# One flag at the scheduler: the same instructions, ordered by a different simulation

## The chip, the cores and the metric

The program runs on one core of one Trainium2 chip, in one launch. The metric is the device time of one execution in microseconds (us). Lower is better. An execution has five instruction streams that matter here: TensorE (PE in the rows, with its weight loads as PEld), VectorE (DVE), ScalarE (ACT), GpSimd (POOL) and SyncE (SP), from which this kernel issues every transfer. Each stream is executed in the order in which it was written into the program; an instruction that waits holds back what stands behind it in its own stream.

## The reference, cut to what matters

One inference step of a two-layer decoder trunk, for a prompt of 1024 tokens and for 8 single-token samples that share the weights. All data is float32. Cut:

```python
def even_layer(hn, ...):                      # layer 0
    u = hn @ w_in                             # q|k|v|gate + z|xBC|dt
    o = dilated_attention(q, k, v)            # three windows: 128/1, 512/4, 2048/16
    att = o * silu(g_att)
    xbc = causal_conv(xbc, ...)               # 4 taps, silu
    y = ssd_scan(xs, dt, a, bm, cm, ...)      # chunks of 128 tokens, a state per head
    y = rmsnorm(y * silu(z))
    return concat([att, y]) @ w_out

def odd_layer(hn, ...):                       # layer 1
    u = hn @ w_in                             # q|k|v|o|i|f|z
    qk = causal_conv(q|k, ...)
    h = mlstm_chunked(q, k, v, i, logf, ...)  # chunks of 128 tokens, a 256x256 memory per head
    h = head_norm(sigmoid(o) * h)
    return (h * silu(z)) @ w_out

# x + even_layer(rmsnorm(x)), then + odd_layer(rmsnorm(.)), then a last rmsnorm;
# the sample tokens take one step each from their caches and states
```

## The kernel before, in words

Activations lie transposed, features on the 128 partitions and the 1032 tokens (1024 of the prompt and 8 samples) along the free axis. To keep float32 accuracy every large product is made of three matmuls: each operand is split into a rounded high part and a low part (`split`, L90: ScalarE casts the high part, VectorE or GpSimd subtracts to get the low part), and `mm3` (L104) adds high x high, high x low and low x high into one PSUM bank. Nearly all of TensorE's time goes into such triples.

PSUM has eight banks of 128x512: three belong to the tag "mm" (`MM`, L72, with `PS_MM = 3`) for the large projections, five to the tag "ax" (`X`, L75) for everything small. A bank is free again when ScalarE or VectorE has read the result.

The program is traced as straight-line code, in this order:

- **Layer 0.** After the first loads and the first norm come the q|k|v blocks (`pq`, 4 groups of 9 blocks), with attention pieces (`att_a`, `att_b`) put between them by hand; then 12 feature tiles through the convolution (`conv_c`, `conv_taps` L243, `conv_act`), then 12 gate tiles (`gate_c`, L228) with the 16 pieces of the state scan (`ssd_prep`, L722, and `ssd_main`) between them, then the output projection (`out_f`, L914) in two halves of the tokens.
- **Layer 1.** Eight heads in a loop (L1496). Each head has four q and k tiles through `conv_c` and two z tiles through `gate_c` (3 pieces of 344 tokens each, result tile `pf`), and then nine blocks: `vo_block` (L1445: 24 matmuls of 512 columns into `pvo`) followed by `mstage` (L1472), which makes the preparation of chunk c (`ml_prep`, L1265), the main part of chunk c-1 (`ml_main`, L1296) and the output of chunk c-2 (`ml_out`, L1330). During head 0 the scalar gates of all heads are made in steps (`gates_a` to `gates_f`), which the loop drops between the projection pieces. Then comes the second output projection and the last norm.

`ml_main` carries the chain from chunk to chunk: the matmuls `mC` give the update of the memory `Cst` (VectorE, L1318), ScalarE rounds it to `mCh` (L91), GpSimd makes the low part `mCl` (L92), and the matmuls `mN` of the next chunk read both:

```python
        if c < 7:
            hd["Cs"] = (R("mCh", [128, 2, VC], 1), R("mCl", [128, 2, VC], 1))
            split(*hd["Cs"], Cst, G)
```

Weights come through the class `Weights` (L116): a transfer into one of three buffers `raw`, a cast `wh` on ScalarE (L91) and a subtraction `wl` on GpSimd or VectorE (L92). `wv_fetch` (L1439) does the same for the v and o weights (`wvh`, `wvl`, the low part always on GpSimd).

What sets the order of the work: the traced order is only the wish. When the block `with tile.TileContext(nc)` closes, a list scheduler plays the whole program through on a simulated machine. Whenever an engine of that machine is free, the scheduler gives it, among the instructions whose inputs are there and for whose tiles a buffer is free at that moment of the simulation, the one that was traced first. The order in which each engine took its instructions becomes the stream of the real engine, and buffers are handed out in the same sequence. So an instruction is moved behind a later-traced one only if the simulated machine finds it not ready. The simulated machine of the kernel before takes the durations of instructions from a static table.

## Time and profile before

| | |
|---|---|
| Time, median of 3 runs | 2216.33 us (2213.23 to 2218.28) |
| The profiled execution's own time | 2213.76 us |
| its span, first to last instruction | 2211.7 us |
| TensorE busy | 2117.2 us of the span (96%) |
| weight loads (PEld) busy | 1890.8 us (85%) |
| VectorE, ScalarE, GpSimd busy | 62%, 38%, 39% |
| mean granted clock of TensorE | 0.986 |
| moved by DMA | 232.29 MB, 105 GB/s |

The span is what the profiler saw between the first and the last instruction; the execution's own time is 2.1 us longer. Matmul records overlap (the engine is pipelined), so "busy" says that at least one matmul was under way, not that the engine ran at its peak. The granted clock is 1.00 where TensorE ran at 2.4 GHz throughout, and falls toward 0.50 in stretches where it ran at 1.2 GHz.

### The profile page before, as it was taken

To read this page: it belongs to the slowest core of one execution; us is meant where nothing else is said; L and a number is where in the kernel's file an instruction comes from. 1 tells how busy PE (TensorE), PEld (TensorE's weight loads), DVE (VectorE), ACT (ScalarE), POOL (GpSimd) and SP (SyncE) were. 2 spreads that over 40 slices of the span, in tenths; PEclk is the share of its full clock that TensorE was granted. 3 is DMA by queue.
4 is the path that set the end of the run, shared out by engine and by line. 5 is a ranking of instruction groups with operands and counts; after the bars stand their busy time and mean duration, and the time that the engine had idled before them with its cause. 6 is when DMAs were issued, how large, how long until landed. Compare 5 with 4: busy or idle time off the path is not lost. (4 is left out here: it accounts for less than half of the span.)

```text
span 2211.7 us, 35220 instructions
## 1 busy us (share of the span) xinstructions
PE 2117.2 (96%) x12913; PEld 1890.8 (85%) x12913; DVE 1381.0 (62%) x3075; ACT 845.4 (38%) x1828; POOL 857.7 (39%) x1167
## 2 busy tenths in 40 slices
PE   7999989998999999899999999999999999999998
PEld 6877777997898798789988889898898988987798
DVE  7344488678877545644648566576575664856854
ACT  5434434454434323433424334243343342523331
POOL 4222152115543343343444435434354344542321
PEclk9999999999999999999999999999999999999999
DMA  4222142325555551411213223132241232415753
GB/s 156 70 73 76 52 145 73 93 71 174 166 183 185 159 175 40 94 37 48 88 33 109 77 89 123 36 102 82 75 138 28 84 104 61 139 38 187 256 179 101
DMA packets 161918, 232.29 MB, mean 105 GB/s; under 512 B 41170, under 2 KB 106690, under 8 KB 161746
## 3 DMA queue, kind: packets, MB, share of 16 engines
q1 hardware_dynamic: 161746, 230.04, 33.2%
q8 instruction: 102, 1.67, 0.3%
q14 instruction: 70, 0.57, 0.1%
HBM read 174.35 MB, written 55.62 MB: 104 GB/s over the span
## 5 line engine op out<-in xcount | busy, mean ns | idle before, releaser
L113 PE MATMUL pf<-yh,wh 128*128 128x344 f32 x1152 | 375.5, 326 | 11.9 <-ACT gth L232 11.0
L113 PE MATMUL pf<-yl,wh 128*128 128x344 f32 x1152 | 372.7, 323 | 1.7 <-POOL yl L92 1.7
L113 PE MATMUL pf<-yh,wl 128*128 128x344 f32 x1152 | 371.5, 323 | 0.3 <-DVE wl L92 0.3
L92 POOL TENSOR_TENSOR wl<-raw,wh 128x1024 fp32r<-128x1024 f32 x86 | 214.6, 2495 | 353.6 <-ACT wh L91 353.6
L113 PEld LDWEIGHTS pf<-yh,wh 128*128 128x128 f32 x1152 | 219.6, 191 | 16.6 <-ACT gth L232 13.5
L113 PEld LDWEIGHTS pf<-yl,wh 128*128 128x128 f32 x1152 | 219.6, 191 | 2.6 <-POOL yl L92 2.6
L113 PEld LDWEIGHTS pf<-yh,wl 128*128 128x128 f32 x1152 | 219.2, 190 | 0.8 <-DVE wl L92 0.7
L246 DVE SCALAR_TENSOR_TENSOR cout<-craw,mcw,cout 128x1024 f32<-128x1024 f32 x96 | 145.7, 1518 | 114.7 <-ACT cout L244 113.1
L91 ACT CAST wh<-raw 128x1024 fp32r<-128x1024 f32 x128 | 134.1, 1048 | 207.6 <-PE po L927 82.0
L113 PE MATMUL pvo<-wvh,yh 128*128 128x512 f32 x512 | 205.8, 402 | 0.0
L113 PE MATMUL pvo<-wvl,yh 128*128 128x512 f32 x512 | 201.7, 394 | 0.0
L113 PE MATMUL pvo<-wvh,yl 128*128 128x512 f32 x512 | 201.6, 394 | 0.0
L113 PE MATMUL pf<-xh,wh 128*128 128x344 f32 x576 | 195.8, 340 | 2.7 <-ACT gth L232 2.7
L113 PE MATMUL pf<-xl,wh 128*128 128x344 f32 x576 | 188.0, 326 | 0.0
L113 PE MATMUL pf<-xh,wl 128*128 128x344 f32 x576 | 187.7, 326 | 0.0
L1263 DVE TENSOR_SCALAR mx<-mx,mbs,md 128x256 f32<-128x256 f32 x64 | 26.4, 413 | 178.0 <-POOL md L1262 178.0
L927 PE MATMUL po<-oh,wl 128*128 128x512 f32 (+2 forms) x384 | 123.6, 322 | 5.2 <-DVE wl L92 4.2
L927 PE MATMUL po<-oh,wh 128*128 128x512 f32 (+2 forms) x384 | 123.9, 324 | 1.0 <-ACT oh L91 1.0
L927 PE MATMUL po<-ol,wh 128*128 128x512 f32 (+2 forms) x384 | 123.1, 321 | 0.0
L113 PEld LDWEIGHTS pf<-xh,wh 128*128 128x128 f32 x576 | 110.8, 192 | 8.8 <-issue 4.9
L92 POOL TENSOR_TENSOR wvl<-raw,wvh 128x1024 fp32r<-128x1024 f32 x32 | 85.5, 2674 | 78.1 <-ACT wvh L91 78.1
L113 PEld LDWEIGHTS pvo<-wvh,yl 128*128 128x128 f32 x512 | 96.1, 188 | 22.3
(435 smaller groups left out, 5307.0 us busy)
## 6 DMA issues: line engine op xcount, KB each, us to landing
raw<-in_wo SPq DMA_DIRECT2D x56, 512.0 KB
raw<-in_wq SPq DMA_DIRECT2D x32, 512.0 KB
raw<-in_wvo SPq DMA_DIRECT2D x32, 512.0 KB
dC<-in_mcs SPq DMA_DIRECT2D x32, 512.0 KB
out_mcs<-dC SPq DMA_DIRECT2D x32, 512.0 KB
raw<-in_wf SPq DMA_DIRECT2D x24, 512.0 KB
sE<-acd SPq DMA_DIRECT2D x16, 512.0 KB
raw<-in_wz SPq DMA_DIRECT2D x16, 512.0 KB
```

Source lines behind the costliest of these rows:

```text
L91: A.copy(hi, src)
L92: eng.tensor_tensor(lo, src, hi.bitcast(F32), sub)
L113: PE.matmul(out, l, r, start=i == 0, stop=i == n - 1)
L246: V.scalar_tensor_tensor(o[:, :NP], raw[:, j : j + NP], w4[:, j : j + 1], o[:, :NP], mult, add)
L927: PE.matmul(p[:, :m], wt[:, ws], at, start=i == 0 and q == 0, stop=i == nk - 1 and q == 2)
L1263: V.tensor_scalar(x, x, bs[:, 6:7], d[:, 2:3], sub, mult)
```

## The change

The scheduler's simulated machine is replaced: instead of the one with the static table of durations it plays the program on an event-driven simulation that has engines, their sequencers, and queues as devices that instructions hold and wait for. The rule of choice (ready, then first traced), the traced program, the tiles, the number of buffers and every instruction's operands stay the same. What can differ is the order of each of the five streams, which buffer of a tag a tile gets, and with these the semaphore waits.

```diff
@@ -1838,7 +1838,7 @@
         I[n] = nc.dram_tensor("in_" + n, a.shape, F32, kind="ExternalInput").ap()
     for n, shape in OUTS.items():
         O[n] = nc.dram_tensor("out_" + n, shape, F32, kind="ExternalOutput").ap()
-    with tile.TileContext(nc) as tc, ExitStack() as ctx:
+    with tile.TileContext(nc, schedule_with_timeline_sim=True) as tc, ExitStack() as ctx:
         body(ctx, tc, I, O)
     r = run_bass_kernel_spmd(nc, [feed], core_ids=[0])
```

## Rows read from the trace of the kernel before

**Rows 1.** The page's first part: busy us, share of the span, instructions.

```profile
PE 2117.2 (96%) x12913; PEld 1890.8 (85%) x12913; DVE 1381.0 (62%) x3075; ACT 845.4 (38%) x1828; POOL 857.7 (39%) x1167
```

**Rows 2.** Span and mean granted clock of the core.

```profile
core 0: 2211.7 us, clock 0.986
```

**Rows 3.** By stretch: length, PE, PEld, DVE, ACT, POOL busy, clock, DMA share, GB/s.

```profile
0.00:45.00 45.00, 29.30 (x150) 26.21 (x151) 32.79 (x84) 23.69 (x53) 21.48 (x40) 1.00 0.58 192
45.00:285.00 240.00, 236.56 (x1469) 187.14 (x1468) 109.10 (x470) 98.03 (x320) 56.17 (x140) 1.00 0.24 70
285.00:345.00 60.00, 51.00 (x316) 43.32 (x316) 53.47 (x98) 23.71 (x63) 34.46 (x17) 0.92 0.46 131
...
520.00:600.00 80.00, 70.93 (x486) 62.09 (x485) 66.53 (x108) 35.93 (x102) 42.97 (x53) 0.96 0.51 166
...
890.00:925.00 35.00, 24.75 (x147) 23.74 (x146) 30.61 (x56) 12.88 (x20) 14.45 (x10) 0.92 0.37 86
...
1100.00:1900.00 800.00, 781.75 (x4597) 711.15 (x4597) 494.16 (x1158) 296.24 (x609) 356.94 (x548) 1.00 0.26 82
...
2195.00:2211.70 16.70, 8.03 (x65) 7.40 (x64) 8.40 (x25) 0.42 (x1) 1.95 (x3) 0.83 0.38 129
```

**Rows 4.** TensorE's waits: us in total, times, longest us.

```profile
PE pf L113 <- ACT gth L232: 13.7, 10, 2.7
...
PE pmb L1207 <- DVE mp L1200: 5.8, 1, 5.8
...
PE pcb L741 <- ACT sbt L745: 5.5, 4, 3.1
...
PE mH L1336 <- DVE mx L1263: 5.4, 11, 1.1
...
PE pgl L1197 <- DVE gp L1191: 3.4, 1, 3.4
```

**Rows 5.** Waits of the other engines, the two longest in total.

```profile
POOL wl L92 <- ACT wh L91: 353.6, 64, 13.7
DVE mx L1263 <- POOL md L1262: 178.0, 64, 3.6
```

**Rows 6.** Timeline of VectorE around 918 us: start, us, instruction.

```profile
918.21 2.32 DVE L1200 TENSOR_TENSOR mp<-mp,btot 1x8 f32<-1x8 f32 x1
...
920.75 2.07 DVE L1200 TENSOR_TENSOR mp<-mp,btot 1x8 f32<-1x8 f32 x1
...
923.04 0.15 DVE L1200 TENSOR_TENSOR mp<-mp,btot 1x8 f32<-1x8 f32 x1
```

**Rows 7.** Timeline of GpSimd in the same stretch.

```profile
918.14 2.37 POOL L92 TENSOR_TENSOR wvl<-raw,wvh 128x1024 fp32r<-128x1024 f32 x1 [5.56 <-ACT wvh L91]
920.46 2.34 POOL L92 TENSOR_TENSOR wl<-raw,wh 128x1024 fp32r<-128x1024 f32 x1
```

**Rows 8.** The convolution taps, L246: duration ns min/median/max, first and last start.

```profile
L246 DVE SCALAR_TENSOR_TENSOR cout<-craw,mcw,cout x96: 1270/1285/3498, 872.6 to 1920.4; 128x1024 f32<-128x1024 f32 x96
```

**Rows 9.** The chain that ended last, one chunk of the last head: start, us.

```profile
1964.74 5.57 PE pvo L113 x24
...
1970.97 1.08 PE mN L113 x9
1972.06 0.72 PE mC L113 x6
...
1973.00 5.58 PE pvo L113 x24
```

**Rows 10.** Groups of instructions: count, busy us, mean ns, idle before.

```profile
L92 POOL TENSOR_TENSOR wvl<-raw,wvh 128x1024 fp32r<-128x1024 f32 x32 | 85.5, 2674 | 78.1 <-ACT wvh L91 78.1
...
L92 POOL TENSOR_TENSOR mCl<-Cst,mCh 128x516 fp32r<-128x516 f32 x56 | 74.7, 1334 | 67.9 <-ACT mCh L91 67.8
...
L1318 DVE SCALAR_TENSOR_TENSOR Cst<-Cst,scl,mC 128x258 f32<-128x258 f32 x112 | 48.6, 477 | 0.0
...
L91 ACT CAST mCh<-Cst 128x516 fp32r<-128x516 f32 x56 | 34.3, 612 | 10.6 <-DVE Cst L1316 8.6 <-DVE Cst L1318 2.0
```

## The prediction, made before the changed kernel ran

> **What bounds the kernel now.** I read the page's first part first. TensorE is busy for 2117.2 us of 2211.7, 96% [rows 1], and no other engine is above 62%, so the time is TensorE's work plus its idle time plus what a low clock takes. The change leaves the work alone, instruction for instruction. Only the other two can move. Idle: 2211.7 - 2117.2 = 94.5 us. Clock: the mean granted is 0.986 [rows 2], so 1.4% of 2211.7 = 31 us of the clock was not granted.
>
> The windows by stretch say where the idle time lies [rows 3]. The start (0 to 45 us: 45 - 29.3 = 15.7 us) waits for the first loads and the first norm, and the end (2195 to 2211.7: 8.7 us) is the last norm and its stores; no order makes these short. That leaves 94.5 - 15.7 - 8.7 = 70.1 us in the middle: 9.0 at 285 to 345, 9.1 at 520 to 600, 10.3 at 890 to 925, 18.3 in the 800 us from 1100 to 1900, and the other 23 us in the stretches not shown and in 45 to 285 (3.4). Layer 1, half the kernel, runs at 781.75 of 800 (98%): there is little to win there and much to lose. Where TensorE stalled the clock fell too: 0.92, 0.96 and 0.92 in the three short stretches against 1.00 in the long ones.
>
> Then TensorE's waits [rows 4]. I chose those in which a matmul of one small chain stands at the head of the stream, or a projection waits for its bank, while other triples could have run: `pf` for the ScalarE reading of the bank before (13.7 us, 10 times), `pmb` (5.8) and `pgl` (3.4) of the gates for VectorE, `pcb` of the state scan (5.5), `mH` (5.4). Together 33.8 us. Each is an instruction placed where the simulated machine thought its input would be there. The longest waits of the other engines have the same form [rows 5]: VectorE stood 64 times, 178.0 us in all, behind `md`, three one-column instructions of GpSimd, and GpSimd 353.6 us behind a cast. They cost nothing by themselves, as these engines have time, but what stands behind them in the stream (readings of PSUM banks among them) is late, and TensorE waits for that.
>
> **The change part by part.** It removes no instruction and adds none, so the sum is over what is moved.
>
> 1. *Small chains go behind triples that are ready.* If the new simulation sees the true length of such a chain, its next matmul is placed later and projection matmuls fill the time one by one. I credit two thirds of the 33.8 us, 22 us: not all, because the filler needs a free bank and split weights. The bounds: nothing, if the stalls only change place, and all 70 us of the middle.
> 2. *The clock.* Of the 31 us the end takes 17% of 16.7 us = 2.8, so 28 us belong to the rest. If about a third of the stalls go (22 of 70), a third of this goes, 9 us; bounds 0 and 28.
> 3. *New waits.* Streams in another order make stalls that are not there now. Nothing in the trace of before shows one. The lower bound is nothing; the upper is worked out under the rivals. I take 5 us, about the 5.4 that `mH` has now.
> 4. *Transfers and buffers.* Every transfer is issued by SyncE, whose stream is reordered too, and the three `raw` buffers go to whichever load the simulation starts first. I cost it at nothing: the DMA engines are at a share of 0.24 to 0.51 in the middle stretches [rows 3], and a weight buffer is loaded a tile ahead. Without that cover a late buffer would cost a wait like the longest of TensorE's in these rows, 5.8 us, each time.
>
> Net: 22 + 9 - 5 = 26 us. From the execution's own time, 2213.8 - 26 = 2188 us. That time is 2.5 us under the median of the runs shown, 2216.3, which is within their spread; against the median it is -1.3%.
>
> One row shows what an order can do that a table of durations doesn't hold. `gates_d` makes the stabilisers with 1x8 instructions on VectorE; one takes 0.15 us, but the two at 918.21 and 920.75 took 2.32 and 2.07 us [rows 6], and in just these stretches GpSimd ran a weight subtraction of 2.37 and one of 2.34 us [rows 7]. `pmb` waited 5.8 us for that. The taps of the convolution show the same stretching: 1285 ns as a median, up to 3498 [rows 8].
>
> The Trainium skill, page "GPSIMD Engine Reference", section "1. Specifications", says that GpSimd's SBUF interfaces are shared with VectorE and contended for by VectorE instructions with two SBUF inputs. The trace agrees, with the 2.32 us beside 0.15. By that rule an order that packs GpSimd tighter makes more such meetings, and the last rival below is worked out for it.
>
> **The rivals.**
>
> *More goes than I credit.* Two thirds of both idle and lost clock in the middle, 65 of 98 us: 2149 us. For it: the waits of the other engines [rows 5] are far longer than TensorE's, so all lateness may come from placement. Against it: 285 to 345 is held by VectorE (53.47 of 60 us), which no order shortens. The weight loads are busy for only 85% of the span [rows 1] and 78% of 45 to 285 (187.14 of 240), where matmuls are recorded as 99% busy [rows 3]; so small matmuls between the large ones cost more there than the idle time shows. The Trainium skill, page "Perfetto Trace Analysis", section "Identifying the Most-Contended Engine", says that the busy share of matmuls is a bad measure and that of weight loads a better one. By it the room is 15% and not 4%.
>
> *Nothing to speak of.* The order is fixed by the data and the trace, stalls change place: 2212 to 2221. For it: a chunk of layer 1 runs exactly in its written order without a gap [rows 9]. Against it: 33.8 us of waits that are plain misplacements.
>
> *Slower: GpSimd's stream delays the chain of layer 1.* From one `pvo` block to the next it is 1973.00 - 1964.74 = 8.26 us [rows 9]. The chain from chunk to chunk is `mC` 0.72, two updates of `Cst` at 0.477, `mCh` 0.612, `mCl` 1.334, `mN` 1.08 us [rows 9, 10]: 4.70 us, and 3.56 to spare. A weight subtraction on GpSimd takes 2.67 us [rows 10]. The scheduler puts any ready one on an idle GpSimd, however little it is needed. One in front of `mCl` fits; two, 5.35 us, exceed the spare time by 1.79, and TensorE has little else to do in a chunk. With two in 28 of the 56 chunks: 50 us, against the 26 gained elsewhere: 2213.8 + 50 - 26 = 2238; in all 56, 2288. It decides from 26 / 1.79 = 15 chunks on. For it: such subtractions fall into these stretches now. Against it: the new simulation would see this delay as well, if its durations are right.
>
> *Slower: TensorE runs ahead and takes the banks.* Once matmuls are pulled forward, the three "mm" banks are opened early and read late; each such `pf` wait is 13.7 / 10 = 1.4 us now. With 40 more of them than now, and the gain of step 1 still made: 2188 + 55 = 2243. It decides from 26 / 1.4 = 19 more on. For it: `pf` for `gth` is already the largest of TensorE's waits. Against it: at 16 gate tiles in layer 1 and 12 in layer 0, 40 more is above one a tile.
>
> *More meetings of GpSimd and VectorE, still faster.* If the two chains of gates are both hit again (5.8 + 3.4 us), and nothing is gained on them, the 33.8 us shrink to 24.6, two thirds are 16, and the 9.2 us become worse by as much again: 2213.8 - 16 - 9 + 5 + 9 = 2203.
>
> **How the numbers follow.** Chances: my forecast 0.35 (2164 to 2200, likeliest 2188), more gained 0.12, nothing to speak of 0.12, GpSimd's chain 0.20, banks 0.13, meetings 0.08. A measurement of this kernel tells a change from none at about 0.2%, 4.4 us. So faster is 0.35 + 0.12 + 0.08 = 0.55, the same 0.12, slower 0.33. As both signs hold much, the range for 8 in 10 must reach into both: at 2150 it leaves out the better half of the first rival (0.06), at 2255 the worse third of the slower ones (0.11). If it is faster, 2150 to 2208.
>
> I have the forecast on the faster side because what is wrong in the present order is of one kind (an instruction placed where its input is late), and if the new simulation's durations are closer to the chip's, which nothing here shows yet, they act on just that. What speaks against more than 1 or 2% is the 98% of layer 1.
>
> **What would show it.** Right: `pmb`, `pgl` and `pf` for `gth` shrink among TensorE's waits; VectorE's 178.0 us behind `md` fall, as other work is put between; the idle time of 520 to 600 and 890 to 925 goes, the granted clock rises above 0.99; the work from 1100 to 1900 takes no longer than now. Wrong: TensorE idle above 94.5 us, with `mN` waiting for `mCl` (the chain), or `pf` for ScalarE (the banks); a layer 1 whose chunks are longer than 8.26 us; or streams that stall in other places for as long as now.

## The result and the profile after

The changed kernel takes 2192.88 us (median of 4 runs, 2190.78 to 2201.33), the kernel before 2215.74 us beside it (4 runs, 2213.23 to 2218.28). The ratio is 0.990 with a 95% interval of 0.9881 to 0.9919: faster by 22.9 us (1%). The median is 4.9 us above the forecast of 2188, and inside the range. The profiled execution has a span of 2191.1 us, 20.6 less than before.

The page's first part and the clock of the changed kernel, to be read beside [rows 1, 2]:

```profile
PE 2113.1 (96%) x12913; PEld 1893.1 (86%) x12913; DVE 1393.3 (64%) x3075; ACT 846.6 (39%) x1828; POOL 883.9 (40%) x1167
```

```profile
core 0: 2191.1 us, clock 0.987
```

TensorE's idle time went from 94.5 to 2191.1 - 2113.1 = 78.0 us, its busy time from 2117.2 to 2113.1; the clock hardly moved. The same stretches as in [rows 3], in the changed kernel:

```profile
285.00:345.00 60.00, 53.88 (x317) 43.67 (x315) 45.86 (x93) 22.90 (x63) 34.36 (x17) 0.94 0.47 137
520.00:600.00 80.00, 77.53 (x580) 67.80 (x581) 72.38 (x127) 42.21 (x124) 49.09 (x60) 1.00 0.61 193
890.00:925.00 35.00, 35.00 (x227) 34.40 (x227) 31.89 (x67) 16.40 (x26) 11.10 (x8) 1.00 0.36 76
1100.00:1900.00 800.00, 796.38 (x4743) 729.52 (x4742) 526.22 (x1189) 309.88 (x630) 387.77 (x566) 1.00 0.27 86
```

Fixed stretches hold other work after a change of order, so I also cut both spans at the same events: the first `pf` of layer 1, the end of the last `pvo` of head 0 and of head 7, the end of the last `po`. Windows of the kernel before, in that cut (layer 0; head 0; heads 1 to 7; last projection; end):

```profile
0.00:836.80 836.80, 789.77 (x5061) 688.48 (x5061) 542.94 (x1215) 349.26 (x859) 281.97 (x353) 0.98 0.40 123
836.80:1005.30 168.50, 155.92 (x882) 139.15 (x881) 99.21 (x256) 58.79 (x133) 71.89 (x111) 0.94 0.22 54
1005.30:2001.50 996.20, 977.20 (x5753) 890.63 (x5753) 612.16 (x1396) 374.34 (x765) 448.90 (x667) 1.00 0.26 82
2001.50:2201.40 199.90, 192.59 (x1214) 171.28 (x1212) 120.47 (x192) 62.61 (x71) 54.23 (x37) 0.99 0.55 184
2201.40:2211.70 10.30, 1.67 (x13) 1.31 (x11) 6.19 (x17) 0.42 (x1) 0.70 (x1) 0.72 0.60 207
```

The same five of the changed kernel:

```profile
0.00:848.10 848.10, 799.29 (x5061) 696.94 (x5061) 538.03 (x1216) 347.90 (x859) 288.15 (x353) 0.98 0.39 122
848.10:1011.40 163.30, 152.80 (x881) 137.59 (x881) 102.20 (x256) 59.02 (x133) 73.80 (x111) 0.95 0.22 56
1011.40:1985.30 973.90, 968.55 (x5753) 886.67 (x5752) 626.09 (x1394) 376.55 (x766) 467.16 (x667) 1.00 0.26 84
1985.30:2175.90 190.60, 188.55 (x1198) 168.56 (x1196) 118.62 (x187) 62.75 (x71) 52.83 (x35) 1.00 0.57 190
2175.90:2191.10 15.20, 3.95 (x27) 3.32 (x26) 8.39 (x25) 0.42 (x1) 1.95 (x3) 0.62 0.41 140
```

Layer 0: +11.3; head 0: -5.2; heads 1 to 7: -22.3; last projection: -9.3; end: +4.9; together -20.6 us. The gain is in layer 1, which I had called almost full, and layer 0, where two of the three stalled stretches of [rows 3] lie, became longer: by 9.5 us of *busy* time of TensorE, with the same instructions.

TensorE's waits in the changed kernel, beside [rows 4] (us in total, times, longest):

```profile
PE pf L113 <- ACT gth L232: 9.2, 7, 3.8
PE pf L113 <- ACT craw L238: 9.1, 3, 5.4
...
PE pmb L1207 <- DVE mp L1200: 5.0, 1, 5.0
PE pf L113 <- ACT yh L91: 5.0, 1, 5.0
...
PE mH L1336 <- DVE mx L1263: 0.6, 3, 0.2
```

(`gth` and `craw` are ScalarE's readings of gate and convolution banks, `yh` its cast of what layer 1 multiplies.) `pcb` and `pgl` are not among them any more; the three groups of `pf` were 13.7, 1.0 and under 1.0 before. All of TensorE's listed waits together went from 86.9 to 71.2 us: groups that shrank gave 45.1, groups that are new or grew took 29.4. Of the other engines, beside [rows 5]:

```profile
POOL wl L92 <- ACT wh L91: 327.7, 69, 10.7
DVE mx L1263 <- POOL md L1262: 166.1, 58, 3.8
```

### The profile page after: what moved, and what is told of

It reads as the page before. It is cut to its first block, busy times and chain, and to the rows that moved or that the text cites. A ratio compares the mean times of both kernels' runs of the same rounds, so it can differ in the third digit from the quotient of the medians.

```text
span 2191.1 us, 35252 instructions
## 1 busy us (share of the span) xinstructions
PE 2113.1 (96%) x12913; PEld 1893.1 (86%) x12913; DVE 1393.3 (64%) x3075; ACT 846.6 (39%) x1828; POOL 883.9 (40%) x1167
## 4 chain that ended last, share of the span: by engine, by line
PE 71%; DVE 15%; DMA 5%; issue 4%; POOL 3%; ACT 2%; SPq 0%; POOLq 0%; DVEq 0%; ACTq 0%
PE pf L113 23%; PE pvo L113 14%; PE po L927 13%; PE pq L113 6%; DVE cout L246 3%; PE mN L113 3%; PE pS L424 2%; DVE dnum L1402 2%; PE mC L113 2%; DVE dC L1398 1%; PE pvo L1465 1%; PE pO L483 1%; PE pT L466 1%; PE mS L1275 1%; DVE cout L251 1%
## 5 line engine op out<-in xcount | busy, mean ns | idle before, releaser
L246 DVE SCALAR_TENSOR_TENSOR cout<-craw,mcw,cout 128x1024 f32<-128x1024 f32 x96 | 141.6, 1477 | 72.5 <-ACT cout L244 71.2
L1263 DVE TENSOR_SCALAR mx<-mx,mbs,md 128x256 f32<-128x256 f32 x64 | 26.4, 412 | 166.3 <-POOL md L1262 166.1
L113 PEld LDWEIGHTS pf<-xl,wh 128*128 128x128 f32 x576 | 110.8, 192 | 4.6 <-issue 4.5
```

Source lines behind the costliest of these rows:

```text
L113: PE.matmul(out, l, r, start=i == 0, stop=i == n - 1)
L246: V.scalar_tensor_tensor(o[:, :NP], raw[:, j : j + NP], w4[:, j : j + 1], o[:, :NP], mult, add)
L1263: V.tensor_scalar(x, x, bs[:, 6:7], d[:, 2:3], sub, mult)
```

## The experiments

An order can be written into the program: after the trace, each instruction of a stream is chained to the one before it in a recorded order, by a dependency that makes no wait on the chip. "Old" and "new" are the orders of the kernel before and of the changed one; layer 1 begins with instruction 8580. Streams and stretches that are not named stay with the scheduler, which places them anew around those that are held. In the programs the orders are packed lists; the cuts below give the rule by which each was made. Common to all kernels with an order:

```diff
         body(ctx, tc, I, O)
+        _at = {int(i.name.split("-")[1]): i for i in nc.cur_bb.bb.instructions if i.name.startswith("I-")}
+        for _l in ORDER.values():
+            for _p, _q in zip(_l, _l[1:]):
+                tc.add_manual_dep(_at[_q], _at[_p].name, _mb.DependencyInfo(_mb.DependencyClass.NoSync, _mb.DependencyReason.DATA), reason="order")
```

### Which layer, which stream

**Layer 0 old, the rest new.**

```diff
+ORDER = {e: [n for n in old[e] if n < 8580] for e in (PE, ACT, DVE, POOL, SP)}
```

> The flag's kernel with all five streams of layer 0 held to the order that they had before; layer 1 and what follows are ordered by the new simulation. By the two traces the flag's layer 0 ends 11.3 us later than before and everything behind it is 31.9 us shorter. If the regions add up: 2192.9 - 11.3 = 2181.6 us. Rival (a late layer 0 is made good behind it, the regions don't add up): 2190 to 2195 us.

2185.93 us, ratio 0.986 (0.9846 to 0.9875): 7 us under the changed kernel, so layer 0's new order does cost time. That is less than the 11.3 of the two profiles. Later profiles show why: layer 0 in its old order took 836.8, 840.5, 841.8 and 843.2 us in four kernels that share it, and in its new order 848.1, 846.3, 845.2 and 846.9 in four others; means 840.6 and 846.6. The loss is about 6 us, and in the two profiles that I had compared the one of before was the shortest of its four, the other the longest.

**Layer 0 new, the rest old.**

```diff
+ORDER = {e: [n for n in old[e] if n >= 8580] for e in (PE, ACT, DVE, POOL, SP)}
```

> The counterpart: layer 0 ordered by the new simulation, all five streams of layer 1 and of the last projection held to the order before. If the regions add up: 2215.7 + 11.3 = 2227 us. Rival (they don't): 2213 to 2218 us.

2228.04 us, ratio 1.0047 (1.003 to 1.0064), 12.3 us above the kernel before. Heads 1 to 7 took 996.2 and the last projection 199.9 us, as before to the tenth: these two stages take the time of their order, whatever layer 0 did. Head 0 doesn't: it took 176.0 us in the old order, 7.5 more than before, with `pmb` waiting 10.9 us and `pf` for `yh` 5.0. So the number 2227 came out, but by the means above only about half of the loss is layer 0's own.

**Only TensorE old from layer 1 on.**

```diff
+ORDER = {PE: [n for n in old[PE] if n >= 8580]}
```

> The flag's kernel, with TensorE's stream alone held to the order before from layer 1 on; the other four are free. My theory, that the gain comes from TensorE's small matmuls being put behind ready triples: the 31.9 us are lost, 2225 us. Rival, that the gain comes from the other engines' streams, which now read PSUM banks sooner: it stays, 2193 to 2197 us.

2223.7 us, ratio 1.003 (1.0018 to 1.0043): the gain is lost, as my theory had it.

**Only TensorE new from layer 1 on**, with the old scheduler.

```diff
-    with tile.TileContext(nc, schedule_with_timeline_sim=True) as tc, ExitStack() as ctx:
+    with tile.TileContext(nc) as tc, ExitStack() as ctx:
+ORDER = {PE: [n for n in new[PE] if n >= 8580]}
```

> The kernel before (scheduled with the static table), with TensorE's stream alone from layer 1 on held to the order that the flag gave it. My theory: 2215.7 - 31.9 = 2184 us. Rival, the other engines' streams carry the gain: 2213 to 2218 us.

2209.88 us, ratio 0.9968 (0.9957 to 0.9979): neither number. TensorE's new order is needed for the whole gain and is not enough for it. In heads 1 to 7 the parts nearly add up: 996.2 us with both old, 984.0 with only TensorE new (-12.2), 987.8 with only the others new (-8.4), 973.9 with both (-22.3). In the last projection they don't: 199.9, 208.5, 200.5 and 190.6; either part alone gains nothing or loses, and the two together gain 9.3. One limit: the four free streams are not the old or the new ones word for word, since their scheduler had to place them around TensorE's held stream. By the starts in the traces, with only TensorE new about a hundred of the 969 instructions of ScalarE from layer 1 on stand elsewhere than in the kernel before. "Others old" and "others new" name the simulation that placed them.

TensorE's waits in heads 1 to 7 show two different stalls. Kernel before:

```profile
PE pf L113 <- ACT gth L232: 11.0, 9, 2.2
PE mH L1336 <- DVE mx L1263: 4.4, 10, 1.1
PE mN L113 <- POOL mCl L92: 2.6, 3, 1.0
```

TensorE old, the others new:

```profile
PE mH L1336 <- DVE mx L1263: 5.1, 7, 1.5
PE mN L113 <- POOL mCl L92: 4.3, 5, 1.3
PE pf L113 <- ACT gth L232: 2.3, 3, 0.8
```

TensorE new, the others old:

```profile
PE pf L113 <- ACT gth L232: 10.3, 9, 2.0
PE mH L1336 <- DVE mx L1263: 0.2, 1, 0.2
```

The waits in the small chain (`mH`, `mN`) go with TensorE's order: where it is new, the next head's `pf` matmuls and the six `mC` stand between the two halves of `mN` of a head's last chunk. The wait of `pf` for a full bank goes with the simulation that placed the others.

**What makes the banks late.** In front of the reading of a gate bank ScalarE stood at an instruction that needs a result of VectorE (4.37 us at L276 around 1490 us in the kernel before; elsewhere at the tanh L250), and VectorE had put updates of the sample memories (`dC`, `dnum`) in front of that result: 30 such places over six heads in the old order, 12 in the new. This run takes them out of the old order; in the last projection it also puts the weight cast in front of `dC` on ScalarE.

```diff
+ORDER = {e: old[e] for e in (PE, ACT, DVE, POOL, SP)}
+ORDER[DVE] = moved(L268..L270, in_front_of=(L1398, L1402), past=30)
+ORDER[ACT] = moved(L231 + L232, in_front_of=L250, times=8) + moved(wh, in_front_of=dC, times=6)
```

> The kernel before, all five streams in its own order but for three kinds of places from layer 1 on. VectorE: the three small instructions that finish a sample's convolution (L268 to L270) go in front of the updates of the sample memories (L1398, L1402) that stand right before them, 30 places in all over six heads (in the changed kernel's order 12 of those stand there). ScalarE: the reading of a gate bank (L231, L232) goes in front of the tanh of the convolution (L250) eight times; in the last projection the weight cast goes in front of the scaling dC (L1394) six times. TensorE's order is the old one. My theory (banks and weights are late because their ScalarE instruction stands behind one that waits for VectorE or for a transfer): most of the pf gaps of heads 1 to 7 (13.7 us above the changed kernel's) and the 4.2 us of po for wl go: 2216 - 9 - 4 = 2203 us (2199 to 2208). Rival (the waits only change place, since TensorE's order has no other work there): 2213 to 2219.

2234.03 us, ratio 1.0075 (1.006 to 1.009): slower, which neither expected. By stages both hold something. Heads 1 to 7 took 989.9 us, 6.3 less (I had said 9); matmul starts to next start, `pf` went from 499.9 to 493.5 us there, against 483.5 in the changed kernel, so the two moves together remove a part of the `pf` stall and not all of it. They were not tested one by one, and only VectorE's tells the two orders apart: the reading of the gate bank stands right behind the tanh in all eight heads before, and still in seven of them in the changed kernel. The last projection took 223.7, 23.8 more. TensorE's and VectorE's waits of this kernel there:

```profile
PE po L927 <- DVE wl L92: 23.0, 3, 9.9
...
DVE dC L1398 <- ACT dC L1394: 30.6, 3, 12.9
```

ScalarE's timeline at one of them:

```profile
2091.55 1.05 ACT L91 CAST wh<-raw 128x1024 fp32r<-128x1024 f32 x1 [4.51 <-PE po L927]
2092.51 3.22 ACT L1394 ACTIVATE dC<-dC,dss 128x1024 f32<-128x1024 f32 x3
```

The cast itself waits for TensorE, which must free its buffer (4.51 us). `dC` now stands behind it, VectorE waits for `dC`, and in VectorE's stream the `wl` that TensorE needs next stands behind that. An order that is right for one stream is wrong for the other two.

### Layer 0: parted pairs

The attention scores `pS` come as two matmuls of 64 rows, one for each head, traced side by side. TensorE's timeline of the kernel before, two places (each instruction leaves two records; read the start of the next instruction):

```profile
83.47 0.70 PE L424 MATMUL pS<-kT,qT 64*128 64x256 f32 x4
84.11 0.45 PE L113 MATMUL pq<-w1h,xh 128*128 128x388 f32 x1
...
101.99 1.28 PE L424 MATMUL pS<-kT,qT 64*128 64x256 f32 x4
103.20 0.44 PE L466 MATMUL pT<-ident,P 128*128 128x128 f32 x2
```

Changed kernel, one head alone:

```profile
115.48 1.27 PE L424 MATMUL pS<-kT,qT 64*128 64x256 f32 x2
116.68 0.44 PE L113 MATMUL pq<-w1h,xl 128*128 128x388 f32 x1
```

A pair holds TensorE for 0.64 or 1.21 us; one head alone holds it for as long, 1.20 here, and 0.63 at 274.92 us of the kernel before. In the trace the two heads of a pair start some 7 ns apart: they run at the same time if they stand together, and one after the other if not. Both are recorded as busy, at a clock of 1.00. In the old order 4 of 128 score instructions stand alone, in the new one 37 (presumably the simulation saw a bank come free for one head and issued it; no run shows why). From the start of each `pS` to the next matmul it is 53.6 us in the old order and 66.6 in the new.

**Pairs joined**, all else new.

```diff
+ORDER = {e: [n for n in new[e] if n < 8580] for e in (PE, ACT, DVE, POOL, SP)}
+ORDER[PE] = joined(ORDER[PE])
```

> All five streams keep the changed kernel's order, except that in layer 0 the two score matmuls of an attention block (pS of head 0 and of head 1, 64 rows each) stand side by side again on TensorE: the first of a parted pair is moved back to the second. 37 of the 128 score instructions stand alone in the changed kernel, 4 in the kernel before, none here. My theory (parted pairs are the 11 us that layer 0 lost, about 13 us for 33 more lone ones, 0.39 each): 37 x 0.39 = 14.5 us back, about 2178 us (2175 to 2182). Rival (layer 0 lost its time in waits, such as the 5.4 us behind the reading of the convolution's bank, which all stay here): 2190 to 2194.

2180.31 us, ratio 0.9831 (0.9816 to 0.9845): 12.6 us less than the changed kernel. `pS` takes 53.4 us again, and the wait of `pf` for `craw` even grew, from 9.1 to 10.1.

**Fourteen more pairs parted.**

```diff
-pS(head 0), pS(head 1), pq, pq, pq
+pS(head 0), pq, pq, pq, pS(head 1)
```

> As the changed kernel, but 14 more pairs of score matmuls are parted in layer 0 on TensorE: the second is moved behind the next three projection matmuls; 65 instead of 37 score instructions stand alone. Nothing else moves. My theory (0.39 us for each lone one): 28 x 0.39 = 11 us more, about 2204 us (2200 to 2211). Rival (parting costs nothing, since the projection matmuls between are wanted anyway): 2190 to 2196.

2209.01 us, ratio 0.9963 (0.995 to 0.9976): 16.1 us more. Layer 0 of the joined and of the parted kernel, windows up to the first `pf` of layer 1:

```profile
0.00:838.40 838.40, 785.43 (x5062) 692.18 (x5062) 534.02 (x1216) 346.13 (x859) 288.97 (x353) 0.98 0.39 123
```

```profile
0.00:865.70 865.70, 822.83 (x5061) 710.81 (x5061) 536.62 (x1216) 349.74 (x859) 288.07 (x353) 0.97 0.38 119
```

The time follows the number of lone ones. In the joined kernel `pS` gives back 66.6 - 53.4 = 13.2 us, 0.36 for each of the 37, and the kernel gains 12.6. In the parted one `pS` takes 77.6 us, 11.0 more, 0.39 for each of the 28, which is the 11 us of the theory. The other 5 of the 16.1 us are not the price of a lone one: layer 0 had a granted clock of 0.97 there instead of 0.98, and no run tells what lowered it. With joined pairs layer 0 took 838.4, 834.5 and 833.1 us in three kernels, mean 835.3, 11.3 under the new order's 846.6 and about 5 under the old order's 840.6. So without the parting the new order seems to gain a little in layer 0 too, though the single values overlap (the lowest of the old ones is 836.8).

### The end, the best kernel, and two prices

**The end old.** In the changed kernel the statistics of the last norm stand behind more `po`, and its second `dg` behind eight scalings `fin` on VectorE.

```diff
+ORDER = {e: [n for n in old[e] if n >= 22840] for e in (PE, ACT, DVE, POOL, SP)}
```

> As the changed kernel, but the end of the program (the last feature of the second output projection and the last norm, on all five engines) in the order of the kernel before. My theory: from the last po to the end it takes 15.2 us in the changed kernel and 10.3 before, since the statistics of the last tokens' first part stand behind more projection matmuls and the diagonal dg of the second part behind eight scalings on VectorE; so 4.9 us come back, 2188 us (2186 to 2190). Rival (the end only takes up time that the last projection gave, which is given back): 2191 to 2194.

2194.35 us (2186.63 to 2194.9), ratio 0.9889 (0.9871 to 0.9907). In the profile, which is of the fastest execution, the end took 10.2 us and the last projection 193.2, together 203.4 against 205.8. So 2.4 us at most, and the executions spread too far to see them: the rival was nearer.

**Pairs joined and the end old.**

```diff
+ORDER = joined pairs, and old[e] for n >= 22840
```

> The edits of the runs with joined pairs and with the old end together, the rest in the changed kernel's order. If both are additive: 2193 - 14.5 - 4.9 = 2173 us (2170 to 2178). Rival (either gives nothing): 2178 to 2190.

2178.56 us, ratio 0.9827 (0.9813 to 0.9841): 1.8 us under joined pairs alone, where 4.9 were expected. The ranges of the two kernels overlap (2177.68 to 2181.65 and 2178.43 to 2179.76), so a gain of the old end is not shown.

**The same with the moves of layer 1**, on the new order.

```diff
+ORDER[DVE] = moved(L268..L270, in_front_of=(L1398, L1402), past=12)
+ORDER[ACT] = moved(L231 + L232, in_front_of=L250, times=8)
```

> The run with joined pairs and the old end, and also the same moves on VectorE (12 places) and of the eight gate readings on ScalarE in layer 1. The heads of the changed kernel have 5.3 us left in pf gaps. If the theory holds here too: 2178.6 - 4 = 2175 us (2172 to 2177). Rival (nothing left to win): 2178 to 2180.

2171.96 us (2170.49 to 2179.84), ratio 0.9802 (0.9782 to 0.9822): 6.6 us less, and the fastest here, 20.9 us under the changed kernel. Heads 1 to 7 took 969.4 us, against 972.5 in the run before, with TensorE busy for 967.9 and no wait of `pf` for `gth` there. So 3.1 us are the moves' by place. Another 3.1 lie in head 0 (164.7 against 167.8), where `pmb` waited 5.1 instead of 7.1 us, and that wait varies between kernels that share its order. The intervals of the two ratios overlap a little.

**The meeting of GpSimd and VectorE by itself.** A block in front of the changed kernel:

```diff
+        for i in range(24):
+            V.tensor_tensor(s, s, t, ALU.add)
...
+        for i in range(12):
+            G.tensor_tensor(c, a, b, ALU.subtract)
+        for i in range(24):
+            V.tensor_tensor(s, s, t, ALU.add)
```

> The changed kernel with a block in front that measures the meeting of GpSimd and VectorE by itself: 24 instructions of VectorE on 1x8 elements and 3 taps of 128x1024 alone, then 12 subtractions of 128x1024 on GpSimd with 24 instructions of 1x8 and 6 taps beside them. My theory (a VectorE instruction with two inputs does not start or end while a GpSimd subtraction runs): alone 0.15 us and 1.27 to 1.29; beside GpSimd about 2.1 to 2.4 us for each 1x8 until the 12 subtractions are through, one for each of them, and taps up to 3.5. Rival (the two slow ones of the kernel before had another cause, such as their PSUM operand or a semaphore): 0.15 us beside GpSimd too.

VectorE's timeline, alone and then beside GpSimd (1x8 elements each; the second row holds six):

```profile
36.52 1.47 DVE L1841 TENSOR_TENSOR ms<-ms,mt 1x8 f32<-1x8 f32 x8
...
38.21 7.23 DVE L1848 TENSOR_TENSOR ms<-ms,mt 1x8 f32<-1x8 f32 x6
```

GpSimd's timeline in the same execution:

```profile
9.27 15.80 POOL L92 TENSOR_TENSOR w1l<-raw,w1h 128x776 fp32r<-128x776 f32 x1 [8.33 <-ACT w1h L91]
...
25.54 1.81 POOL L92 TENSOR_TENSOR w1l<-raw,w1h 128x776 fp32r<-128x776 f32 x1
38.26 7.17 POOL L1846 TENSOR_TENSOR mcc<-ma,mbb 128x1024 fp32r<-128x1024 f32 x3 [10.91 <-DVE ma L1844]
```

Eight took 1.47 us alone; beside three subtractions six took 7.23, two for each (the time of this kernel, 2244.29 us, holds the block and tells nothing): the one that meets a subtraction takes 2.2 us, the next slips in between at 0.15. So a meeting is enough to make such an instruction slow. That it was the cause in `gates_d` is shown by its two kinds of 1x8 instructions, which alternate on VectorE. Both inputs of L1200 lie in SBUF; L1199 reads `pgl` from PSUM. In the changed kernel (duration ns min/median/max, first and last start):

```profile
L1199 DVE TENSOR_TENSOR mp<-mp,pgl x8: 144/150/152, 923.9 to 936.3; 1x8 f32<-1x8 f32 x8
L1200 DVE TENSOR_TENSOR mp<-mp,btot x8: 153/155/4769, 924.0 to 936.5; 1x8 f32<-1x8 f32 x8
```

Only L1200 is ever slow, here and in the kernel before (151 and 2324 ns at most). The page "GPSIMD Engine Reference" of the Trainium skill, section "1. Specifications", says that GpSimd's SBUF interfaces are shared with VectorE and that VectorE instructions with two SBUF inputs contend for them; the trace agrees. The probe's taps had been scheduled ahead of its twelve subtractions; they met an earlier one and took 1.27 us each, while that subtraction waited (last section). The taps of the kernel itself show both ways: before, one took 3.50 us (at 1777.71) beside a subtraction of 2.37, and at 1206.06 one took 1.28 beside a subtraction that took 3.49.

**The price of a late `mCl`.** Four more subtractions of its size behind each `mCl`, all streams in the new order.

```diff
             split(*hd["Cs"], Cst, G)
+            for _ in range(4):
+                G.tensor_tensor(hd["Cs"][1], Cst, hd["Cs"][0].bitcast(F32), sub)
```

> The changed kernel, all streams in its order, with the low part mCl subtracted four times more on GpSimd in each of the 56 chunks: 4 x 1.334 = 5.35 us in the chain from chunk to chunk, what two weight subtractions would cost there. By the prediction's rival 3.56 us of a chunk were to spare, so 1.79 us too many: 56 x 1.79 = 100 us more, about 2293 us (2270 to 2310); mN waits for mCl in nearly each chunk. Against it (TensorE has matmuls that it can take meanwhile, or the chain has more to spare): under 2230.

2481.3 us, ratio 1.1196 (1.1172 to 1.122): 288 us more, 288 / 56 = 5.15 for each chunk, of 5.35 that were put in. `mN` waited for the last of the subtractions in all 56 chunks:

```profile
PE mN L113 <- POOL mCl L1323: 194.0, 56, 6.0
```

Timeline of VectorE, of GpSimd and of TensorE in one chunk:

```profile
1155.71 0.41 DVE L1263 TENSOR_SCALAR mx<-mx,mbs,md 128x256 f32<-128x256 f32 x1 [8.76 <-POOL md L1262]
1156.04 0.42 DVE L92 TENSOR_TENSOR mvl<-pvo,mvh 128x256 fp32r<-128x256 f32 x1
...
1158.88 0.47 DVE L1318 SCALAR_TENSOR_TENSOR Cst<-Cst,scl,mC 128x258 f32<-128x258 f32 x1
```

```profile
1149.04 5.40 POOL L1323 TENSOR_TENSOR mCl<-Cst,mCh 128x516 fp32r<-128x516 f32 x4
1154.52 0.22 POOL L1260 TENSOR_SCALAR md<-md 128x1 f32<-128x1 f32 x1
```

```profile
1150.84 0.28 PE L113 MATMUL mC<-mvh,mkh 128*128 128x258 f32 x1
...
1164.28 0.28 PE L113 MATMUL mC<-mvh,mkh 128*128 128x258 f32 x1
```

The loop from chunk to chunk is longer than the data say: `md` stands behind `mCl` in GpSimd's stream, `mx` waits for `md`, and in VectorE's stream `mvl`, `mA`, `mkl` and both `Cst` stand behind `mx`; on ScalarE `mCh` stands behind the exponential of `mE`, and GpSimd's step before that one waited 0.93 us for a transfer here. The pitch of a chunk here is 1164.28 - 1150.84 = 13.44 us between equal `mC` matmuls; less 5.36 (four times 1.34) that is 8.08, against 8.26 [rows 9]. By this chunk and by the mean of all 56 about 0.2 us are to spare, not 3.56. That is an estimate: only one amount was put in, and the granted clock fell to 0.95 in this kernel (0.987), of which a part of the 5.15 may come. In the chunk shown the update of `Cst` starts 1.6 us after TensorE's last `mC`, so there the loop does not hang on TensorE.

## Why the forecast held, and where it did not

The forecast was 2188, the median is 2192.88. The size came out nearly right, but by other ways than I gave, and in part by luck. Cut by the sum's terms: idle time was to fall by 22 - 5 = 17 us and fell by 16.5; the clock was to give 9 us, and TensorE's busy time, in which the clock shows, fell by 4.1. In these 4.1 a rise of 9.5 in layer 0 and 2.3 in the end stands against a fall of 15.8 in the stages between, and the sum had a term for neither.

1. *Small chains go behind ready triples: 22 of 33.8 us.* The five groups are at 9.2 + 5.0 + 0.6 us now, 19.0 less; the size was right, and so were the signs `pf`, `pgl`, `mH` (VectorE's wait behind `md` fell only from 178.0 to 166.1). The groups that I had not chosen gave another 26.1, which I had put at nothing. And I gave one mechanism, a matmul placed too early in TensorE's stream. The runs with one part old show that this holds for `mH` and `mN`; the wait of `pf` for `gth`, the largest group, shrank with the other streams. One likely part is that VectorE had 12 instead of 30 memory updates in front of a small result that ScalarE waited for; the run that took all 30 out moved ScalarE's readings as well, so this part alone is not shown.
2. *The clock: 9 us.* Mis-sized. (1 - 0.987) x 2191.1 = 28.5 us are still not granted, 2.5 less than 31. The clock rose in 520 to 600 and 890 to 925, as I had said, but the mean stayed at 0.987 and did not rise above 0.99, the sign that I had given: head 0 as a whole stayed at 0.95 (0.94 before), layer 0 at 0.98, and the end, longer now, fell from 0.72 to 0.62.
3. *New waits: 5 us.* The step that failed most. Waits that are new or grew make 29.4 us: `pf` for `craw` 8.1 more, `pf` for `yh` 5.0, the rest in pieces under 3. That the net of idle time came out all the same is luck: these 24 us too few and the 26.1 us that I had left out of step 1 cancel. The end is 4.9 us longer. And the dearest single loss was not a wait. I had looked for what a new order can cost only in idle time, and the parted pairs cost 12.6 us in time that is recorded as busy. It is what I had noted for the rival with more gain, small matmuls that cost more than the idle time shows, with the other sign.
4. *Transfers and buffers: nothing.* In the last projection `po` no longer waits 4.2 us for `wl`. Before, the cast of those weights stood on ScalarE behind a scaling of sample memories that waited 5.17 us for its transfer; in the changed kernel the two scalings in front of it waited 0.97 and 1.44 us. It is not chance: over the whole kernel the scalings `dC` waited 49 to 63 us for these transfers in the four kernels whose other streams from layer 1 on come from the static table, and 12 to 21 where they come from the new simulation. Whether SyncE's order or a buffer did it was not told apart; no run held SyncE's stream alone.

*Layer 1 has little to win.* Wrong. I read 98% busy as 2% of room. Heads 1 to 7 lost 13.7 us of idle time (19.0 to 5.35) and 8.65 of busy time (977.2 to 968.55), the latter with a cause that stays open. The work from 1100 to 1900 takes no longer, as I had said; it became shorter.

*The rivals.* GpSimd's chain did not happen: in both kernels GpSimd's weight subtractions within the nine blocks of a head all start in its first 6 us, ahead of the head's first `mCl` (at 15.6 us or later), so what I had put down for it was wrong. Its price was wrong too, in the other direction: by the estimate above, with 0.2 instead of 3.56 us to spare, already one subtraction of 2.67 us would cost about 2.5, and some ten chunks (26 / 2.5) would have decided. The banks: `pf` for ScalarE's readings rose from 14.7 (13.7 + 1.0) to 18.3 us (9.2 + 9.1), at 10 places as against 12, far from 40 more. The meetings: there are three in `gates_d` now and not two (4.77, 2.13 and 2.08 us), the longest beside two subtractions, yet `pmb` waits 5.0 us. VectorE and GpSimd of the changed kernel:

```profile
924.05 4.77 DVE L1200 TENSOR_TENSOR mp<-mp,btot 1x8 f32<-1x8 f32 x1
```

```profile
924.00 4.79 POOL L92 TENSOR_TENSOR wvl<-raw,wvh 128x1024 fp32r<-128x1024 f32 x2
```

`pgl` went, so of the 9.2 us of this rival 5.0 are left and nothing was added. What a meeting costs changes with its moment: over the kernels of this document `pmb` waits from 4.8 to 10.9 us. *Nothing to speak of* (2212 to 2221) is refuted by the interval. *More goes than I credit* (2149) is not what the flag does; the best order found by hand, 2172, lies two thirds of the way to it.

What stays open: the other part of the `pf` stall in layer 1 (493.5 us with the moved instructions, 483.5 in the changed kernel), which stream gives the last projection its 9.3 us, and whether the new simulation's durations are closer to the chip's, which nothing here measured. The 5 us that `pf` waits for `yh` at the start of layer 1 come from layer 0's new order: 5.0 us with layer 0 new and the rest old, 1.1 with layer 0 old and the rest new.

## What to carry to other kernels

A scheduler whose order is faster as a whole can still part two instructions that are worth more side by side: after a change of order, compare start to next start for each kind of small matmul, not only idle time, and keep pairs together that can run at once. Cut both spans at the same events before looking for a gain, and price a chain along the streams (what stands behind the waiting instruction on its engine), not along the data alone. To repair one wait, don't move an instruction that itself waits for the engine that is to be helped in front of work that others need: the weight cast of the slower run did just that. And a forecast whose sum comes out is not yet a forecast whose terms did: compare them one by one.

## What the hardware showed that I had not expected

GpSimd can be held up as well as VectorE (times of GpSimd in a profile are rough): a subtraction of 128x776 that takes 1.81 us took 15.80 in the probe, while VectorE ran its taps and small instructions from 9.3 to 23.3 us without a gap; a 1x8 on VectorE then took 1.77 us, and the subtraction ended with it. Two score matmuls of 64 rows each cost TensorE no more than one: 1.21 us for the pair, 1.20 for one alone.
